# Conditioning matmuls of a decoder block in whole visits from a ring of their own

## The chip, the cores and the metric

One core of a Trainium2 chip runs the whole kernel. The metric is the device time of one execution in microseconds (us); lower is better. The times before are 1353.8, 1354.12 and 1354.7 us, with a median of 1354.12. All views below are of one other execution, taken by the hardware profiler: it took 1353.11 us, of which 1351.3 us lie between its first and its last instruction (the span).

## The reference, cut to what matters

One layer of a decoder trunk runs on 288 token columns: 256 of a prompt, and 32 of eight samples with four tokens each. All numbers are 32-bit floats.

```
mod = silu(c) @ w_ada + b_ada            # 9 conditions; 6 parts of 2048 columns: sh1 sc1 g1 sh2 sc2 g2
h   = rmsnorm(x)*(1+sc1) + sh1
proj = h @ w_in                          # pooling input u, gate z, xbc (conv + state-space mixer), dt
mix = concat(pool(u), ssd(z, xbc, dt)) @ w_out
x   = x + g1*mix
h2  = rmsnorm(x)*(1+sc2) + sh2
x   = x + g2*((silu(conv(h2 @ w_gate)) * (h2 @ w_val)) @ w_down)
y   = rmsnorm(x)
```

The change is about the first line, the conditioning. It multiplies nine condition vectors by a 2048 x 12288 matrix, 100 MB to be read. Parts 0 and 1 (sh1, sc1) are needed first. Parts 2, 3 and 4 (g1, sh2, sc2) are needed at the output projection and behind it. Part 5 (g2) comes still later.

## The kernel before, in words

Every weight comes from HBM by a DMA that SyncE (SP) issues, mostly 512 KB at a time, into a buffer named `raw` (`load`, L267). A large weight is then split for accuracy into a high part `whi` (ScalarE, ACT) and a rest `wlo` (VectorE, DVE) by `split` (L293). TensorE (PE) runs three matmuls for each 128 x 128 block of it on all 288 columns (`mm3`, L301).

**The rings.** A ring is a fixed number of buffers that loads take in turn; a load waits until the last reader of its buffer is done. Class `_W` (L457) keeps one ring of `raw`, one of `whi` and one of `wlo`, and gives them buffers as memory comes free. Pool `w1` (L485) gives 8 `raw` and 2 of each split buffer for the whole run. Pool `w0` (L502) gives 8 and 1 until the last block of the input projection. Pool `w2` (L1156) gives 1 and 2 from step m == 5 of the output stage on. Conditioning loads and weight loads share the `raw` ring.

**The stages.** Blocks 0 to 5 of the input projection run first, with parts 0 and 1 of the conditioning between them (`ada_group_units`, L352). The last block (bi = 6, 28 steps m) makes the rest of `xbc`. The uz stage (L1038) then makes the remaining z and u in eight steps of eight units. Beside it runs the state-space mixer of four head groups (`back`), whose many small matmuls take turns with the large ones on PE. The output stage (L1087 and L1151) has sixteen steps of 48 large matmuls. The MLP follows.

**The conditioning matmuls.** `ada_part_units` (L405) makes one part. For each of 16 slices k of the contraction it loads two chunks of 512 KB and runs four matmuls with 32 columns of weights and 512 columns of data (`ada_mm`, L329). Each of the four has a quarter of the PE array, so that four run side by side. The data is plain fp32 here, not split. A matmul in the program is two matmul records in the profile. With AY = 2 the generator hands back control after every second k, so a part is eight visits of 8 matmuls (16 records). Behind the last, ACT copies the sums out (`ada_sb`, L335), PE transposes them (`ada_tr`, L340), and four DVE instructions add the bias (L420).

**What sets the order.** The program is one list of instructions, and generators place the conditioning between other work: `pull` (L987) counts up a fraction at each step and asks for the next piece when it reaches one. The last block pulls 0.25 a step (L1033), uz 0.2 a unit (L1043); two visits are pulled behind uz (L1051). The output stage pulls 0.5 and later 1 a step (L1167), and what is left is drained at m == 13 (L1169). At build time the framework's scheduler then orders each engine's queue: by program order, but an instruction whose inputs it takes to be late may be overtaken by one that it takes to be ready. `tc.high_priority()` lets an instruction go ahead of others, and `tc.keep_in_program_order` sets it behind the instruction before it on its engine. Parts 0 and 1 use both (L377 to L382), parts 2 to 5 neither. On the chip each engine runs its queue strictly in the order that was fixed.

Of the kernel before, what the change touches and what calls it, by code (L numbers as in the profile page):

```python
# [39 lines left out]
RAW0, RAW1, RAW2 = 8, 8, 1  # L40
# [11 lines left out]
AY = 2  # L52

RA1, RA2, RB1, RB2, RB3 = 0.5, 0.4, 1.0, 1.0, 1.0
TA, ADA_OUT = 4, 4
# [109 lines left out]
def kernel(ctx: ExitStack, tc, ins, outs):  # L165
# [101 lines left out]
    def load(key):  # L267
        off, cols = S.items[key]
        t = wp[0].tile([P, RAWC], F32, tag="raw", name="raw_" + "_".join(map(str, key)))
        nc.sync.dma_start(t[:, :cols], wflat[off:off + P * cols].rearrange("(p n) -> p n", p=P))  # L270
        return t
# [5 lines left out]
    def top_up():  # L277

        while queue and nloads[0] - min((n for n, _ in ahead.values()), default=nloads[0]) < RAW0 + RAW1:
            key = queue.popleft()  # L280
            ahead[key] = (nloads[0], load(key))
            nloads[0] += 1
# [121 lines left out]

    def ada_part_units(part, ay=1):  # L405
        ps = pa.tile([P, 512], F32, tag="ada", name=f"adap{part}")
        for k in range(KT):
            raws = [load(("adap", part, k, h)) for h in range(2)]
            for h in range(2):
                ada_mm(ps, raws[h], k, 0, 512, range(2 * h, 2 * h + 2))  # L410
            if k % ay == ay - 1:
                yield
        asb = ada_sb(ps, 512, f"p{part}")
        yield
        pt = ada_tr(asb, 512, f"p{part}")
        for i in range(4):
            o = ada[:, part].rearrange("p (j i) c -> p j i c", j=4)[:, :, i, :]
            b = bada[:, part].rearrange("p (j i) -> p j i", j=4)[:, :, i]
            src = pt[:, i * P:(i + 1) * P].rearrange("p (j c) -> p j c", j=4)[:, :, 0:NC9]
            nc.vector.tensor_tensor(o, src, b.unsqueeze(2).to_broadcast([P, 4, NC9]), ALU.add)  # L420
        if part == 4:
            ada_scale(1, 4, vec[:, V_N2:V_N2 + KT], 0, KT)
        yield
# [33 lines left out]
    class _W:  # L457


        def __init__(self):  # L460
            self.slots = {"raw": [], "whi": [], "wlo": []}
            self.i = {"raw": 0, "whi": 0, "wlo": 0}

        def add(self, pool, nraw, nsp):
            for tag, n in (("raw", nraw), ("whi", nsp), ("wlo", nsp)):
                m = len(self.slots[tag])
                if m:
                    r = self.i[tag] % m
                    self.slots[tag] = self.slots[tag][r:] + self.slots[tag][:r]
                    self.i[tag] = 0  # L470
                self.slots[tag] += [(pool, n)] * n

        def drop(self, pool):
            for tag, sl in self.slots.items():
                r = self.i[tag] % len(sl)
                self.slots[tag] = [x for x in sl[r:] + sl[:r] if x[0] is not pool]
                self.i[tag] = 0

        def tile(self, shape, dt, tag, name):
            pool, n = self.slots[tag][self.i[tag] % len(self.slots[tag])]  # L480
            self.i[tag] += 1
            return pool.tile(shape, dt, tag=tag, name=name, bufs=n)

    wp[0] = _W()
    wp[0].add(ctx.enter_context(tc.tile_pool(name="w1", bufs=1, side="right")), RAW1, SPLIT1)  # L485
# [16 lines left out]
    wp[0].add(w0, RAW0, SPLIT0)  # L502
# [405 lines left out]
    adas = chain(*(ada_part_units(p, AY) for p in (2, 3, 4)))  # L908
# [86 lines left out]
    for bi in range(len(BLOCKS)):  # L995
        last = bi + 1 == len(BLOCKS)
        top_up()
        if last:

            wp[0].drop(w0)  # L1000
            w0_ctx.close()
            sx[0] = mx_ctx.enter_context(tc.tile_pool(name="sx", bufs=1, reuse_waits="tile"))
            raw = load(("dt",))[:, :KT * NH].rearrange("p (k h) -> p k h", h=NH)
# [11 lines left out]
            late_states()  # L1015
            dt_stage(ps)
# [4 lines left out]
        for i, m in enumerate(xbc_units(bi)):  # L1021
            if not last:
                top_up()
                if bi == 0 and i in (3, 7, 13):
                    ci = {3: 2, 7: 3, 13: 4}[i]
                    ready["xbc", 0, ci] = split(fetch(("xbc", 0, ci)), 0, len(_xbc_chunks(0)[ci][1]) * P,
                                                f"xbc0_{ci}", pin=True)
                if i in VIS[bi]:
                    next(nxt)
                    top_up()  # L1030
            else:
                pull(back, 0.5 if m < 20 else RB1) if m >= 9 else None
                pull(adas, RA1 / AY)  # L1033
# [4 lines left out]
    for m in list(range(4 + 3 * ZEARLY, 16)) + ULATE:  # L1038
        for _ in uz_units(m):
# [3 lines left out]
            pull(adas, RA2 / AY)  # L1043
# [7 lines left out]
    pull(adas, TA / AY)  # L1051
# [36 lines left out]
    for i in range(KT // YK):  # L1088
# [6 lines left out]
        if i == 3:  # L1095
            psq = aux("ysum")
            col_sums(psq, ssq, ones[:, 0:1], True, True)
            _, rstdy = rstd_of(psq, NH * 64, "rstdy")
    mx_ctx.close()
# [51 lines left out]
    for m in range(16):  # L1151
# [15 lines left out]
        pull(adas, (1 + (m >= 14 - ADA_OUT)) / AY)  # L1167
# [3 lines left out]

    adag2 = ada_part_units(5)
# [285 lines left out]
```

## Time and profile before

| what | value |
|---|---|
| median of three runs | 1354.12 us (1353.8 to 1354.7) |
| the profiled execution | 1353.11 us |
| its span | 1351.3 us |
| last block of the input projection | from about 189 to 257 us |
| uz stage with the mixer | about 257 to 373 us |
| output stage | about 373 to 495 us |
| DMA reads from HBM | 309.78 MB |

PE rows are matmuls, PEld rows are weight loads into the array, which overlap them; SPq rows are DMA issues. A row of the timeline gives the start, the time until the end of its last matmul, engine, line, operation, output <- inputs, shapes and the count of like instructions in a row. Matmuls are pipelined, so rows overlap a little, and the distance from start to start is the true step. In a wait table the waiter stands left of the arrow. Rows of "windows" give the busy time of each engine in a stretch, with the count of instructions.

### The profile page before, as it was taken

How to read it: one execution, taken by the hardware profiler on the slowest of the kernel's cores; microseconds unless marked ns; L12 is line 12 of the kernel's file. 1: busy time of each engine (PE TensorE's matmuls, PEld its weight loads, DVE VectorE, ACT ScalarE, POOL GpSimd, SP SyncE). 2: the span in 40 equal slices, each digit the busy share in tenths (PEclk: the TensorE clock that was granted, in tenths of full speed). 3: DMA queues.
4: the chain of work that ended last, by engine and by line, in shares of the span. 5: the costliest groups of instructions: out<-in, count | busy, mean ns of one | idle time of the engine just before them, and what ended most of it. 6: DMA issues, size and time to landing. Idle time of an engine off the chain costs nothing.

```text
span 1351.3 us, 26246 instructions
## 1 busy us (share of the span) xinstructions
PE 1337.3 (99%) x10517; PEld 1247.5 (92%) x10517; DVE 820.0 (61%) x1394; ACT 579.4 (43%) x911; POOL 227.5 (17%) x449
## 2 busy tenths in 40 slices
PE   9999999999999999999999999999999999999997
PEld 8889997776789889999999999999999999999997
DVE  5776568778665568645665445656655556566543
ACT  5343244587733335434443333434433343444442
POOL 0000012122122223111211001321120011132221
PEclk9999999999999999999999999999999999999999
DMA  9999768978888877787555555655555565566531
GB/s 373 405 408 368 252 242 324 340 257 295 324 332 323 320 253 257 249 280 265 181 187 182 162 178 183 204 183 196 181 180 164 184 191 184 187 207 194 179 119 70
DMA packets 97482, 323.19 MB, mean 239 GB/s; under 512 B 10768, under 2 KB 19920, under 8 KB 97360
## 3 DMA queue, kind: packets, MB, share of 16 engines
q1 hardware_dynamic: 93600, 310.79, 66.3%
q0 software_dynamic: 3184, 9.69, 2.0%
q8 instruction: 82, 1.34, 0.4%
q10 hardware_dynamic: 576, 1.03, 0.2%
q14 instruction: 40, 0.33, 0.1%
HBM read 309.78 MB, written 10.39 MB: 237 GB/s over the span
## 4 chain that ended last, share of the span: by engine, by line
PE 74%; DVE 1%; issue 0%; ACT 0%; DVEq 0%
PE mm_down L304 7%; PE mm_down L303 7%; PE mm_down L305 7%; PE mm_gate L303 6%; PE mm_val L304 6%; PE mm_gate L304 6%; PE mm_val L305 6%; PE mm_gate L305 6%; PE mm_val L303 6%; PE adap L332 3%; PE mm_out L303 2%; PE mm_out L304 2%; PE mm_out L305 2%; PE mm_up L303 1%; PE mm_up L304 1%; PE mm_up L305 1%
## 5 line engine op out<-in xcount | busy, mean ns | idle before, releaser
L304 PE MATMUL mm_down<-al,whi_down 128*128 128x288 f32 x688 | 202.5, 294 | 0.0
L303 PE MATMUL mm_down<-ah,whi_down 128*128 128x288 f32 x688 | 202.4, 294 | 0.0
L305 PE MATMUL mm_down<-ah,wlo_down 128*128 128x288 f32 x688 | 202.0, 294 | 0.0
L304 PE MATMUL mm_val<-h2l,whi_val 128*128 128x288 f32 x640 | 189.1, 296 | 0.0
L304 PE MATMUL mm_gate<-h2l,whi_gate 128*128 128x288 f32 x640 | 189.1, 295 | 0.0
L303 PE MATMUL mm_gate<-h2h,whi_gate 128*128 128x288 f32 x640 | 188.8, 295 | 0.0
L305 PE MATMUL mm_val<-h2h,wlo_val 128*128 128x288 f32 x640 | 188.4, 294 | 0.0
L305 PE MATMUL mm_gate<-h2h,wlo_gate 128*128 128x288 f32 x640 | 188.4, 294 | 0.0
L303 PE MATMUL mm_val<-h2h,whi_val 128*128 128x288 f32 x640 | 187.9, 294 | 0.0
L291 DVE TENSOR_TENSOR wlo_gate<-raw_gate,whi_gate 128x1024 fp32r<-128x1024 f32 x80 | 98.4, 1230 | 136.4 <-ACT whi_gate L289 136.3
L291 DVE TENSOR_TENSOR wlo_down<-raw_down,whi_down 128x1024 fp32r<-128x1024 f32 x96 | 107.5, 1120 | 116.9 <-ACT whi_down L289 114.4
L289 ACT CAST whi_down<-raw_down 128x1024 fp32r<-128x1024 f32 x96 | 92.3, 961 | 167.0 <-PE mm_down L304 118.0
L289 ACT CAST whi_gate<-raw_gate 128x1024 fp32r<-128x1024 f32 x80 | 83.8, 1049 | 160.0 <-PE mm_gate L304 64.9
L289 ACT CAST whi_val<-raw_val 128x1024 fp32r<-128x1024 f32 x80 | 84.1, 1051 | 119.5 <-issue 101.9
L303 PE MATMUL xbc<-h1h,whi_xbc 128*128 128x288 f32 x448 | 133.5, 301 | 0.8 <-ACT h1h L453 0.7
L304 PE MATMUL xbc<-h1l,whi_xbc 128*128 128x288 f32 x448 | 132.0, 296 | 0.0
L305 PE MATMUL xbc<-h1h,wlo_xbc 128*128 128x288 f32 x448 | 130.0, 295 | 0.0
L303 PEld LDWEIGHTS mm_down<-ah,whi_down 128*128 128x128 f32 x688 | 129.2, 188 | 0.0
L304 PEld LDWEIGHTS mm_down<-al,whi_down 128*128 128x128 f32 x688 | 129.1, 188 | 0.0
L305 PEld LDWEIGHTS mm_down<-ah,wlo_down 128*128 128x128 f32 x688 | 129.0, 187 | 0.0
L303 PEld LDWEIGHTS mm_gate<-h2h,whi_gate 128*128 128x128 f32 x640 | 120.3, 188 | 5.0 <-ACT ah L1221 3.4
L305 PEld LDWEIGHTS mm_gate<-h2h,wlo_gate 128*128 128x128 f32 x640 | 120.5, 188 | 0.0
(331 smaller groups left out, 2994.8 us busy)
## 6 DMA issues: line engine op xcount, KB each, us to landing
raw_adap<-wflat SPq DMA_DIRECT2D x128, 512.0 KB, 5.6
raw_gate<-wflat SPq DMA_DIRECT2D x80, 512.0 KB, 3.6
raw_val<-wflat SPq DMA_DIRECT2D x80, 512.0 KB, 3.9
raw_ada<-wflat SPq DMA_DIRECT2D x64, 512.0 KB, 9.6
raw_xbc<-wflat SPq DMA_DIRECT2D x50, 512.0 KB, 9.5
raw_down<-wflat SPq DMA_DIRECT2D x48, 512.0 KB, 3.6
raw_out<-wflat SPq DMA_DIRECT2D x32, 512.0 KB, 7.6
raw_down<-wflat SPq DMA_DIRECT2D x32, 384.0 KB, 3.1
```

Of the source, the lines that this page charges most:

```text
L289: yield nc.scalar.copy(hi[:, :n], raw[:, a:a + n])
L291: yield hi, lo, nc.vector.tensor_tensor(lo[:, :n], raw[:, a:a + n], hi[:, :n].bitcast(F32), ALU.subtract)
L303: nc.tensor.matmul(ps, whi[:, w], bh, start=first, stop=False)
L304: nc.tensor.matmul(ps, whi[:, w], bl, start=False, stop=False)
L305: nc.tensor.matmul(ps, wlo[:, w], bh, start=False, stop=last)
L332: nc.tensor.matmul(ps[32 * j:32 * j + 32, :nb], sc_c[:, k, :], raw[:, c:c + nb], start=(k == 0), stop=(k == KT - 1), tile_position=(0, 32 ...
```

## The change

Parts 2, 3 and 4 get a new generator, `ada_visits`. It loads all chunks of a visit, hands back control, and then puts all matmuls of the visit in one piece: the first waits for the chunk that was loaded last, the others have high priority, and all are kept in program order. A visit of parts 2 and 3 holds two slices k (AK = 2: 4 chunks, 8 matmuls, as before). A visit of part 4 holds four (AK2 = 4: 8 chunks, 16 matmuls), so part 4 has four visits in place of eight.

The chunks of these parts get a ring of their own, `rawa`. In the first blocks its four buffers of `w1` still count to the common ring (4 + 4 + 8 buffers, as before). From the last block on they are `rawa`, and weights have four of `w1` and one in pool `sx`, five, in place of eight shared. In the output stage `rawa` has eight buffers, and weights four, in place of nine shared; the additional split buffers come at m == 0 in place of m == 5. For the MLP all twelve are one ring, in place of nine.

Parts 2 and 3 are pulled at 4 x 5.01/28 a step in the last block and 4 x 11.01/62 a unit in uz, with four pulls to a visit: 5 visits and 11. Part 4 runs at the ends of steps 3, 6, 9 and 12 of the output stage; its chunks are asked for one by one in the two steps before each. Nothing is pulled behind uz as a block of its own. The four bias additions of a part become one DVE instruction at high priority, for part 5 too.

```diff
-RAW0, RAW1, RAW2 = 8, 8, 1
+RAW0, RAW1, RAWA, RAW2 = 8, 4, 4, 4
-AY = 2
-RA1, RA2, RB1, RB2, RB3 = 0.5, 0.4, 1.0, 1.0, 1.0
-TA, ADA_OUT = 4, 4
+VA = (5.01 / 28, 11.01 / 62)
+AK, AK2, AOUT = 2, 4, (3, 6, 9, 12)
+RB1, RB2, RB3 = 1.0, 1.0, 1.0
...
+    def ada_visits(parts, step, spread=False):
+        plan = [(part, k0) for part in parts for k0 in range(0, KT, step)]
+        ahead, end = [], None
+        def chunks(v):
+            part, k0 = plan[v]
+            for k in range(k0, k0 + step):
+                for h in range(2):
+                    ahead.append((k, h, load(("adap", part, k, h), "rawa")))
+                    if spread:
+                        yield
+            if not spread:
+                yield
+                yield
+        yield from chunks(0)
+        for v, (part, k0) in enumerate(plan):
+            if end:
+                ada_end(*end)
+                end = None
+            if k0 == 0:
+                ps = pa.tile([P, 512], F32, tag="ada", name=f"adap{part}")
+            n = 0
+            for k, h, raw in ahead[::-1]:
+                for j in (2 * h, 2 * h + 1):
+                    with tc.high_priority() if n else nullcontext():
+                        i = nc.tensor.matmul(ps[32 * j:32 * j + 32, :], sc_c[:, k, :],
+                                             raw[:, 512 * (j % 2):512 * (j % 2) + 512], start=k == step - 1,
+                                             stop=k == KT - step, tile_position=(0, 32 * j))
+                    tc.keep_in_program_order(i)
+                    n += 1
+            ahead.clear()
+            if k0 + step == KT:
+                end = part, ada_sb(ps, 512, f"p{part}")
+            yield
+            if not spread:
+                yield
+            if v + 1 < len(plan):
+                yield from chunks(v + 1)
+        ada_end(*end)
+        yield
...
+    def ada_end(part, asb):
         pt = ada_tr(asb, 512, f"p{part}")
-        for i in range(4):
-            o = ada[:, part].rearrange("p (j i) c -> p j i c", j=4)[:, :, i, :]
-            b = bada[:, part].rearrange("p (j i) -> p j i", j=4)[:, :, i]
-            src = pt[:, i * P:(i + 1) * P].rearrange("p (j c) -> p j c", j=4)[:, :, 0:NC9]
-            nc.vector.tensor_tensor(o, src, b.unsqueeze(2).to_broadcast([P, 4, NC9]), ALU.add)
+        with tc.high_priority():
+            nc.vector.tensor_tensor(ada[:, part].rearrange("p (j i) c -> p i j c", j=4),
+                                    pt.rearrange("p (i j c) -> p i j c", i=4, j=4)[:, :, :, 0:NC9],
+                                    bada[:, part].rearrange("p (j i) -> p i j", j=4).unsqueeze(3)
+                                    .to_broadcast([P, 4, 4, NC9]), ALU.add)
...
-    adas = chain(*(ada_part_units(p, AY) for p in (2, 3, 4)))
+    adas = ada_visits((2, 3), AK)
...
             wp[0].drop(w0)
+            wp[0].move("rawa", "raw", "rawa")
...
+            wp[0].add(sx[0], "raw", "raw", 1)
...
             late_states()
+            next(adas)
             dt_stage(ps)
...
-                pull(adas, RA1 / AY)
+                pull(adas, 4 * VA[0])
...
-            pull(adas, RA2 / AY)
+            pull(adas, 4 * VA[1])
...
-    pull(adas, TA / AY)
+    drain(adas)
...
+    wp[0].drop(sx[0])
     mx_ctx.close()
...
-        if m == 5:
-            wp[0].add(w2, RAW2, SPLIT2)
+        if m == 0:
+            for tag, n in (("rawa", RAW2), ("whi", SPLIT2), ("wlo", SPLIT2)):
+                wp[0].add(w2, tag, tag, n)
+            adas = ada_visits((4,), AK2, True)
...
+                if i % 2 and m < AOUT[-1] and m % 3:
+                    next(adas)
...
-        pull(adas, (1 + (m >= 14 - ADA_OUT)) / AY)
+        if m in AOUT:
+            next(adas)
         if m == 13:
             drain(adas)
+    wp[0].move("rawa", "rawa", "raw")
```

The rest of the diff lets `load` name its ring and rewrites class `_W` so that a buffer can be moved from one ring to another.

More of the change, by code (lines that the diff above doesn't have):

```diff
@@ L277, in top_up @@
     def top_up():
-        while queue and nloads[0] - min((n for n, _ in ahead.values()), default=nloads[0]) < RAW0 + RAW1:
+        while queue and nloads[0] - min((n for n, _ in ahead.values()), default=nloads[0]) < RAW0 + RAW1 + RAWA:
             key = queue.popleft()
@@ L460, in __init__, with turn, add, move @@
         def __init__(self):
[L461 to L471, printed above, removed]
+            self.slots = {"raw": [], "rawa": [], "whi": [], "wlo": []}
+            self.i = dict.fromkeys(self.slots, 0)
+        def turn(self, ring):
+            sl = self.slots[ring]
+            r = self.i[ring] % len(sl) if sl else 0
+            self.slots[ring], self.i[ring] = sl[r:] + sl[:r], 0
+        def add(self, pool, ring, tag, n):
+            self.turn(ring)
+            self.slots[ring] += [(pool, tag, n)] * n
+        def move(self, tag, a, b):
+            self.turn(a)
+            self.turn(b)
+            self.slots[b] += [x for x in self.slots[a] if x[1] == tag]
+            self.slots[a] = [x for x in self.slots[a] if x[1] != tag]
         def drop(self, pool):
[L474 to L477, printed above, removed]
+            for ring in self.slots:
+                self.turn(ring)
+                self.slots[ring] = [x for x in self.slots[ring] if x[0] is not pool]
         def tile(self, shape, dt, tag, name):
-            pool, n = self.slots[tag][self.i[tag] % len(self.slots[tag])]
-            self.i[tag] += 1
+            pool, tag, n = self.slots[tag][self.ix(tag)]
             return pool.tile(shape, dt, tag=tag, name=name, bufs=n)
+        def ix(self, ring):
+            self.i[ring] += 1
+            return (self.i[ring] - 1) % len(self.slots[ring])
     wp[0] = _W()
-    wp[0].add(ctx.enter_context(tc.tile_pool(name="w1", bufs=1, side="right")), RAW1, SPLIT1)
+    w1 = ctx.enter_context(tc.tile_pool(name="w1", bufs=1, side="right"))
+    for ring, tag, n in (("raw", "raw", RAW1), ("raw", "rawa", RAWA), ("whi", "whi", SPLIT1), ("wlo", "wlo", SPLIT1)):
+        wp[0].add(w1, ring, tag, n)
     mx_ctx = ExitStack()
@@ L501 @@
     shift(w0, 32)
-    wp[0].add(w0, RAW0, SPLIT0)
+    for tag, n in (("raw", RAW0), ("whi", SPLIT0), ("wlo", SPLIT0)):
+        wp[0].add(w0, tag, tag, n)
     sx = [None]
```

7 lines of the change are left out of this document (4 added, 3 removed).

## The prediction

> **What bounds the kernel now.** I read the page first, then the waits of PE between 196 and 501 us, where parts 2 to 4 of the conditioning run.
>
> ```profile
> PE 1337.3 (99%) x10517; PEld 1247.5 (92%) x10517; DVE 820.0 (61%) x1394; ACT 579.4 (43%) x911; POOL 227.5 (17%) x449
> ...
> PE 74%; DVE 1%; issue 0%; ACT 0%; DVEq 0%
> ```
> ```profile
> PE cse L801 <- DVE ada L420: 1.0, 1, 1.0
> PE pool L888 <- DVE pout L883: 0.8, 1, 0.8
> PE dttr L582 <- DVE dtt L570: 0.6, 1, 0.6
> PE cb L751 <- DVE xde L740: 0.3, 1, 0.3
> ```
>
> PE is busy for 99% of the span and names the chain that ended last. In these 305 us it waits 2.7 us in four places, and never for a DMA. So no stall of size is to be had. Time can only come from PE work that takes longer than it must: matmuls that don't fill the array, and changes between kinds of matmul. The question is how much of that the conditioning contains, and whether the new rings turn a wait for a DMA into PE time. First a visit that is in one piece, in the output stage:
>
> ```profile
> 397.60 0.29 PE L305 MATMUL mm_outp<-mixh,wlo_out 128*128 128x288 f32 x1
> 397.82 1.92 PE L332 MATMUL adap<-raw_adap,sc_c 128*32 128x512 f32 x16
> 399.68 0.40 PE L303 MATMUL mm_out<-mixh,whi_out 128*128 128x288 f32 x1
> 399.92 0.30 PE L304 MATMUL mm_out<-mixl,whi_out 128*128 128x288 f32 x1
> ```
>
> The visit takes 1.86 us from start to start. From 397.60 to 399.92 are 2.32 us, where two steps of large matmuls would be 0.26 (they follow each other by 0.13). A visit thus costs 2.06 us, of which 0.20 are entry and exit. Now one in uz that the build order has cut in two, and the first piece of another that is cut in three:
>
> ```profile
> 324.92 1.04 PE L332 MATMUL adap<-raw_adap,sc_c 128*32 128x512 f32 x2
> ...
> 332.85 1.92 PE L332 MATMUL adap<-raw_adap,sc_c 128*32 128x512 f32 x14
> ```
> ```profile
> 213.97 1.05 PE L332 MATMUL adap<-raw_adap,sc_c 128*32 128x512 f32 x2
> ```
>
> This is the main reading. Two records alone take 1.04 us, and the fourteen left take 1.92, as long as sixteen. Four matmuls side by side take as long as one, so a piece that isn't a multiple of eight records pays for a whole round of the array, about 0.9 us. From this first one on seven visits are cut, one in three and six in two: eight pieces too many. The last of them is quoted further down, with the joint behind uz.
>
> **The change part by part.** *Tying.* The busy time of these matmuls by stretch:
>
> ```profile
> 196.00:373.00 177.00, 38.44 (x268) 7.72 (x272) 1.18 (x2) 1.00 0.83 305
> 373.00:501.00 128.00, 20.95 (x160) 4.27 (x152) 0.58 (x1) 1.00 0.83 310
> ```
> ```profile
> 496.40 1.04 PE L332 MATMUL adap<-raw_adap,sc_c 128*32 128x512 f32 x2
> ...
> 498.17 2.77 PE L332 MATMUL adap<-raw_adap,sc_c 128*32 128x512 f32 x22
> ```
>
> Together 59.39 us. The first part of part 5 is in it and stays (1.92 + 1.04 + 2.77 = 5.73). The 24 visits of parts 2 to 4, whole, would be 24 x 1.92 = 46.08. The excess is 7.58; the eight pieces overlap what follows by some 0.07 each, which leaves **-7.0**. Each piece also has an entry and exit, 0.2 beside large matmuls and nothing beside other small ones; I take 0.1: **-0.8** (0 to -1.6). That the tie holds is read from the stage before, where parts 0 and 1 have it:
>
> ```profile
> 48.14 1.93 PE L378 MATMUL adag<-raw_ada,sc_c 128*32 128x256 f32 x32
> ```
>
> It is the first of twelve such visits up to the dt stage; each is one row of 32 in the timeline.
>
> *Four long visits.* The row of 22 records is three rounds, so a round is 2.77 - 1.92 = 0.85 us. Four rounds take 3.62, or 3.75 with the overlap taken off and the entry added. Eight visits of 2.05 (16.4) become four of 3.75 (15.0): **-1.4**.
>
> *One addition in place of four.* PE's 1.0 us wait above is for the last of them:
>
> ```profile
> 285.87 0.39 DVE L420 TENSOR_TENSOR ada<-adat_p,early 128x36 f32<-128x36 f32 x3
> ```
>
> The last three of the four stand behind others on DVE, and the PSUM bank that they read is held until the fourth is through. A single one at the head of the queue frees it sooner by at most the wait, 1.0; I take **-0.7** (0 to -1.0), nearer to the whole since nothing is left behind the first. DVE is 61% busy, so the twelve instructions less (0.13 each by this row, part 5 included) give nothing else.
>
> *What goes from the joint behind uz.* Two visits now stand between uz and the output stage, as rows of PE and one of DVE show:
>
> ```profile
> 371.11 0.29 PE L305 MATMUL mm_uz<-h1h,wlo_uz 128*128 128x288 f32 x1
> 371.25 0.60 PE L343 MATMUL adat_p<-early,asb_p 128*128 128x128 f32 x4
> 371.77 1.93 PE L332 MATMUL adap<-raw_adap,sc_c 128*32 128x512 f32 x16
> ```
> ```profile
> 378.59 1.04 PE L332 MATMUL adap<-raw_adap,sc_c 128*32 128x512 f32 x2
> 379.57 0.75 PE L888 MATMUL pool<-pout,poolw 128*128 128x288 f32 x2
> 380.15 0.72 PE L241 MATMUL ysum<-ones,ssq 128*128 128x1 f32 x6
> 380.81 1.92 PE L332 MATMUL adap<-raw_adap,sc_c 128*32 128x512 f32 x14
> ```
> ```profile
> 378.53 0.17 DVE L883 TENSOR_TENSOR pout<-pout,upp 128x16 f32<-128x16 f32 x1
> ```
>
> The last uz matmul is at 371.1; the pooling that hangs on it leaves DVE at 378.7. Between lie 36 large matmuls, and three pieces of conditioning, 4.7 us from start to start, that cover the rest. Without them the large ones end near 376.5, and PE has 2.2 us until the pooling can go on, unless weights of the next step are split by then (their buffers come free after 24 of the 36). I take **+2.0**; the bounds are 0 and the whole cover, 4.7.
>
> *A ring of one visit.* `rawa` holds four chunks, which is just one visit: a load waits on SP until the visit before has read its buffer. What is queued behind it on SP are loads of weights; what is queued behind a visit on PE is everything. How long does a batch take to come? Twice from SP's timeline, each with the landing of its last load from the DMA view of that instant:
>
> ```profile
> 398.92 1.75 SPq L270 DMA_DIRECT2D raw_adap<-wflat  x4
> ```
> ```profile
> raw_adap<-wflat SPq DMA_DIRECT2D x1, 512.0 KB, 6.0
> ```
> ```profile
> 226.86 0.80 SPq L270 DMA_DIRECT2D raw_adap<-wflat  x2
> 227.77 0.84 SPq L270 DMA_DIRECT2D raw_xbc<-wflat  x2
> 228.67 7.39 SPq L270 DMA_DIRECT2D raw_adap<-wflat  x4
> ```
> ```profile
> raw_adap<-wflat SPq DMA_DIRECT2D x1, 512.0 KB, 9.1
> ```
>
> The visit at 397.82 frees its buffers, four loads follow, the last is issued at 400.3 and lands 6.0 later: 8.5 us from visit to full ring. With two weight loads between (the visit at 225.77, fourth load at 229.2, landing 9.1 later) it is 12.5. The visits' distance comes from the stage rows:
>
> ```profile
> 189.00:257.00 68.00, 67.40 (x510) 53.66 (x512) 58.61 (x138) 31.56 (x45) 15.65 (x31) 1.00 0.83 307
> 257.00:373.00 116.00, 113.89 (x916) 83.28 (x912) 82.98 (x161) 88.50 (x199) 24.57 (x35) 1.00 0.82 297
> ```
>
> The last block loses two of its seven visits and a cut: near 63 us, 28 steps, a visit every 5.6: 12.5 us. uz has eleven, near 112 us for 64 units, a visit every 5.6: 9.9 us. So the last block has room, and uz lies between the two reload times. The build order lets other matmuls go first where it sees the batch late; PE stops only by what the chip is later than it. I take **+1.0**, with 0 below; the other end is a rival. The weights' smaller rings I price at nothing: uz uses one 512 KB load in 7 us and has five buffers, the output stage one in 3.2 us with four, 12.7 us of cover, and four split buffers behind. A load there takes 7.6 (median):
>
> ```profile
> raw_out<-wflat SPq DMA_DIRECT2D x32, 512.0 KB, 7.6
> ```
>
> If that cover goes, each late load stops PE for what it is late. Part 4's eight chunks have three steps of 6.3 us and a visit, 22.8 us. Two loads more made 4.0 us of the two reload times, so eight take at most 8.5 + 4 x 2.0 = 16.5 by themselves.
>
> *Sum.* -7.0 - 0.8 - 1.4 - 0.7 + 2.0 + 1.0 = **-6.9 us**. The profiled execution took 1353.1 and would take 1346.2. It lies 1.0 below the median of 1354.1, so I forecast **1347.2**.
>
> **The rivals.** *1. The ring that is reloaded too late (slower).* In uz each visit stands at the head of PE's queue before its last chunk has landed. At 12.5 us of reload against 9.9 of distance, eleven visits wait up to 2.6 each: 28 us. At half of that 14 us, and 1361. It eats the gain from 0.7 us of wait per uz visit on ((6.9 + 1.0) / 11). For it: 297 GB/s already move in that stage, and one batch has no second buffer. Against it: PE waited for no DMA before, and a visit may be moved back. The Trainium skill, Trainium Kernel Development and Optimization, section Best Practices, says: "Double-buffer for performance: Overlap DMA with compute". By that rule a ring of exactly one visit is the wrong size, and this rival would be the likeliest; no row here shows such a ring yet.
>
> *2. The gain is given back at the joint.* The full 4.7 us of cover are missed, and the other terms hold: -4.2, 1349.9. For it: the pooling chain of 7.3 us behind uz (371.4 to 378.7) is DVE's, and nothing in the change shortens it. Against it: weights of step 1 may be ready.
>
> *3. It doesn't do what it says.* New pins move the cuts elsewhere, into the mixer's small matmuls, and pieces stay. Then only the long visits and the joint count, about 0: 1354. Against it is the row of 32.
>
> *4. More than counted.* The joint costs nothing, no batch is late, every entry counts: -7.0 - 1.6 - 1.4 - 1.0 = -11.0, 1343.1.
>
> **How the numbers follow.** Forecast 0.60, its own range 1344 to 1351; rival 1 0.16; rival 2 0.12; rival 3 0.07; rival 4 0.05. The range of 1343 to 1356 leaves out half of rival 4 and most of rival 1. A measurement of this kernel tells about 0.2% from no change, 2.7 us, so faster means below 1351.4 and slower above 1356.8. Faster: the forecast nearly whole, rival 4, half of rival 2: 0.71. Same: the rest of rival 2, most of 3, the mild part of 1: 0.14. Slower: 0.15.
>
> **What would show it.** Right: visits as single rows of 16 (1.9 us) and four rows of 32 (3.6) after each third output step; busy time of these matmuls near 51 us between 196 and 501; no wait of DVE's addition; a gap of up to 2 us before the pooling behind uz. Wrong: waits of PE for a chunk, or of the `whi` casts for weights that then reach PE; rows of 2 or 6 records; visits that slip behind uz.

## The result, and the profile after

The changed kernel takes 1357.69 us (median of 16 runs, 1355.96 to 1359.64), the kernel before beside it 1353.70 us (16 runs, 1352.58 to 1354.70). The ratio is 1.003, with a 95% interval of 1.0023 to 1.0038. The change makes the kernel slower by about 4 us, where 1347.2 had been forecast. The profiled execution took 1357.75 us, of which 1355.9 are the span.

First come the two lines of the page after that answer to those of before: busy time, and the chain that ended last.

```profile
PE 1332.5 (98%) x10517; PEld 1247.9 (92%) x10517; DVE 823.0 (61%) x1382; ACT 577.8 (43%) x909; POOL 222.0 (16%) x449
...
PE 90%; DMA 5%; DVE 2%; ACT 1%; SPq 1%; issue 1%; POOL 0%; DVEq 0%; ACTq 0%; POOLq 0%
```

PE is busy for 4.8 us *less* in a span that is 4.6 us longer. So matmul time has gone, and more than that has come as waiting. DMA, which the chain of before did not name, has 5% of the chain. The wait table of PE between 180 and 520 us says where:

```profile
PE mm_out L303 <- ACT whi_out L289: 4.2, 2, 2.2
PE mm_out L305 <- DVE wlo_out L291: 3.3, 4, 1.5
PE adap L432 <- DMA raw_adap<-wflat: 1.2, 2, 1.0
PE pool L946 <- DVE pout L941: 1.1, 2, 0.7
PE cb L809 <- DVE xde L798: 0.8, 2, 0.6
PE cse L859 <- DVE yo L845: 0.4, 1, 0.4
```

The first two rows did not exist before: large matmuls of the output stage wait 7.5 us for the casts that split a weight. The wait of `cse` for the bias addition (`ada`, 1.0) is gone.

What the change did to the visits stands in PE's timeline (start, us, count at the end of the row):

```profile
357.70 1.92 PE L432 MATMUL adap<-raw_adap,sc_c 128*32 128x512 f32 x16
367.45 1.92 PE L432 MATMUL adap<-raw_adap,sc_c 128*32 128x512 f32 x16
...
401.12 3.64 PE L432 MATMUL adap<-raw_adap,sc_c 128*32 128x512 f32 x32
404.69 0.40 PE L303 MATMUL mm_out<-mixh,whi_out 128*128 128x288 f32 x1
```

Every visit of parts 2 and 3 is one row of 16, from 194.75 to 367.45 us, and part 4 is four rows of 32 that take 3.57 us from start to start. Their busy time, in two stretches that meet between two visits (the first number behind the comma is PE's; 1.00 and 0.99 are the mean granted TensorE clock, as a share of the full one):

```profile
194.00:365.00 171.00, 28.86 (x240) 6.26 (x240) 0.59 (x1) 1.00 0.82 301
365.00:505.00 140.00, 22.34 (x184) 5.28 (x184) 1.18 (x2) 0.99 0.86 311
```

That is 51.2 us against 59.39 before. The same from start to start, without the overlaps, gives an account of all that lies between the first matmul of the dt projection and the first of the MLP (`mm_up`). A large matmul follows another by 0.1321 us where nothing is late; what a stretch of them takes beyond that is its loss.

| us | before | after | difference |
|---|---|---|---|
| whole stretch | 315.51 | 319.81 | +4.30 |
| conditioning matmuls, part 5's first pieces among them | 56.93 | 50.04 | -6.9 |
| losses of large matmuls ahead of the output stage | 11.09 | 11.04 | 0.0 |
| losses of large matmuls in the output stage | 1.87 | 12.10 | **+10.2** |
| all other matmuls | 44.77 | 45.80 | +1.0 |

The losses stand in two places: 6.3 us at 385 to 395 us (steps 2 and 3 of the stage), and 4.3 us at 421 and at 441 to 445. (Elsewhere the stage loses a little less than before, since it has fewer visits.) Follow three of the waits back. PE's timeline (in brackets the idle time before a row and what ended it):

```profile
387.44 0.40 PE L303 MATMUL mm_out<-mixh,whi_out 128*128 128x288 f32 x1 [2.05 <-ACT whi_out L289]
...
389.34 0.44 PE L304 MATMUL mm_out<-mixl,whi_out 128*128 128x288 f32 x1
389.58 0.44 PE L305 MATMUL mm_out<-mixh,wlo_out 128*128 128x288 f32 x1
...
394.83 0.40 PE L305 MATMUL mm_out<-mixh,wlo_out 128*128 128x288 f32 x1 [1.54 <-DVE wlo_out L291]
...
443.45 0.40 PE L303 MATMUL mm_out<-mixh,whi_out 128*128 128x288 f32 x1 [2.20 <-ACT whi_out L289]
```

The two rows in the middle wait for nothing, yet follow each other by 0.24 us in place of 0.13. The window of PE there shows why: the granted clock is half.

```profile
388.50:391.70 3.20, 3.00 (x12) 0.50 1.03 401
```

For 3.4 us, from 388.4 on, thirteen large matmuls run at half clock, which costs 1.5 us. So the loss of 12.1 us in the output stage is 7.5 us of waits, 1.5 us of half clock, and 3.1 us in small pieces at waits and visits, where the kernel before has 1.9 in all. The waits came first, and without the stretch at half clock this execution would still have taken about 1356 us. The sixteen executions differ in their mean clock: the six at 0.996, the profiled one among them, took 1355.96 to 1357.75 us, the eight at 0.994 took 1357.68 to 1359.64, and those of the kernel before that ran beside the experiments stand at 0.997 or 0.998. That the slower ones had a further such stretch is not shown, as only one execution was profiled.

ACT's timeline shows that the casts had no choice either; they waited for the load:

```profile
386.34 1.04 ACT L289 CAST whi_out<-raw_out 128x1024 fp32r<-128x1024 f32 x1 [0.37 <-DMA raw_out<-wflat]
...
419.25 1.05 ACT L289 CAST whi_out<-raw_out 128x1024 fp32r<-128x1024 f32 x1 [6.40 <-DMA raw_out<-wflat]
...
442.36 1.04 ACT L289 CAST whi_out<-raw_out 128x1024 fp32r<-128x1024 f32 x1 [5.95 <-DMA raw_out<-wflat]
```

And SP's timeline shows what those loads stood behind, at the start of the stage and after the first long visit:

```profile
368.55 3.10 SPq L270 DMA_DIRECT2D raw_adap<-wflat  x5
371.70 0.95 SPq L1216 DMA_DIRECT2D x<-x  x2
...
373.28 0.40 SPq L270 DMA_DIRECT2D raw_out<-wflat  x1
...
402.21 6.60 SPq L270 DMA_DIRECT2D raw_adap<-wflat  x8
408.91 13.00 SPq L270 DMA_DIRECT2D raw_out<-wflat  x5
```

The code asks for the eight chunks of a visit one by one over two steps. But behind the long visit they stand in SP's queue as one row of eight, ahead of the weights, and go out from 402.21 to 408.16, as the visit at 401.12 frees the buffers. (At the start of the stage it is six chunks and two loads of `x` ahead of the weight at 373.28.) The landing times of the trace: the chunk issued last, at 408.16, lands at 417.87, and the weight issued at 408.91 lands at 419.15. The next three weights land at 420.43, 421.69 and 422.95, one in every 1.27 us. The DMA view of the five weights:

```profile
raw_out<-wflat SPq DMA_DIRECT2D x5, 512.0 KB, 10.1
```

Their median is 10.1 us from issue to landing, where the stage before the change had a median of 7.6. Between 403.64 and 419.15 us no weight lands at all; 15.5 us are nearly five weights' worth of matmuls (one in 3.2 us). Ahead of the two larger groups of waits the gaps are longer: 18.4 us (367.96 to 386.32) and 17.2 us (425.03 to 442.26). Behind the visit at 450.99 the gap is 12.4 us (454.93 to 467.33), less than four weights' worth, and no large matmul waits.

### The profile page after: what moved, and what is told of

Same layout as the page of the kernel before. It is cut to its first block, busy times and chain, and to the rows that moved or that the text cites. A ratio compares the mean times of both kernels' runs of the same rounds, so it can differ in the third digit from the quotient of the medians.

```text
span 1355.9 us, 26197 instructions
## 1 busy us (share of the span) xinstructions
PE 1332.5 (98%) x10517; PEld 1247.9 (92%) x10517; DVE 823.0 (61%) x1382; ACT 577.8 (43%) x909; POOL 222.0 (16%) x449
## 3 DMA queue, kind: packets, MB, share of 16 engines
HBM read 309.78 MB, written 10.39 MB: 236 GB/s over the span
## 4 chain that ended last, share of the span: by engine, by line
PE 90%; DMA 5%; DVE 2%; ACT 1%; SPq 1%; issue 1%; POOL 0%; DVEq 0%; ACTq 0%; POOLq 0%
PE mm_down L304 7%; PE mm_down L303 7%; PE mm_down L305 7%; PE mm_gate L303 6%; PE mm_val L304 6%; PE mm_gate L304 6%; PE mm_gate L305 6%; PE mm_val L305 6%; PE mm_val L303 6%; PE xbc L303 5%; PE xbc L304 4%; PE xbc L305 4%; PE adap L432 3%; DMA raw_out<-wflat 2%; PE adag L378 2%; DMA raw_adap<-wflat 1%
```

## The experiments

The theory: the large matmuls lose time because eight chunk loads go out in one burst ahead of a weight on the one queue, and the rest of the change gives what was forecast. The rivals were that the new ring or the new distances cost something by themselves, that the weights have too few buffers, that SP's standing in the queue (not the bytes) delays the weights, and that visits of eight chunks cost something whatever the order. All ratios are against the kernel before, run beside each.

**part4_as_before.** Part 4 goes back to short visits of four chunks at the old pace, from one common ring, with the additional split buffers at m == 5; parts 2 and 3 stay as changed.

```diff
-            adas = ada_visits((4,), AK2, True)
+            adas = ada_part_units(4, 2)
...
-        if m in AOUT:
-            next(adas)
+        pull(adas, (1 + (m >= 10)) / 2)
...
+    wp[0].move("rawa", "rawa", "raw")
```

> Parts 2 and 3 as in the changed kernel; part 4 as in the kernel before: visits of two slices, four chunks each, from a ring that they share with the weights (8 buffers, 9 from step 5 on, with the additional split buffers from step 5). Theory (the burst of eight chunks after each long visit stands ahead of the weights in the DMA queue, and a ring of four for the weights can't cover it): no wait of PE for a weight cast in the output stage, and what the tied visits won up to the end of uz is left, 4 to 5 us: about 1349. Rival (what uz wins is only work that was moved behind it): 1353 to 1354.

1347.59 us, ratio 0.9955 (0.9941 to 0.9969): 5.9 us below the kernel before, and the fastest of all kernels here. The two largest waits of PE from 180 to 520 us:

```profile
PE pool L946 <- DVE pout L941: 1.1, 2, 0.7
PE adap L432 <- DMA raw_adap<-wflat: 1.0, 1, 1.0
```

No large matmul waits for a cast. Their loss in the output stage is 2.33 us, and the conditioning takes 49.99. SP issues four chunks and then four weights:

```profile
395.70 3.19 SPq L270 DMA_DIRECT2D raw_adap<-wflat  x4
398.98 5.46 SPq L270 DMA_DIRECT2D raw_out<-wflat  x4
```

So the loss came with the long visits, and not from the ring or the distances of parts 2 and 3. Which property of the long visits it is, this run alone does not say: it changes their length, their ring and their place.

**short_visits.** The generator, the ring of eight and the split buffers of the change stay; a visit of part 4 holds two slices in place of four, pulled evenly.

```diff
-AK, AK2, AOUT = 2, 4, (3, 6, 9, 12)
+AK, AK2 = 2, 2
...
-                if i % 2 and m < AOUT[-1] and m % 3:
-                    next(adas)
+                pull(adas, 0.39)
...
-        if m in AOUT:
-            next(adas)
```

> The changed kernel with part 4 in eight visits of two slices, evenly over steps 1 to 13; rings as in the changed kernel (eight buffers for chunks, four for weights). A visit frees four buffers, so bursts are half as long, 5 us, but as many bytes are moved. Theory (length of the burst): most waits go, 1347 to 1350, with 1.4 us more for the four additional visits. Rival (ring of four, or total load on the DMA): 1355 or more.

1348.85 us, ratio 0.9964 (0.9951 to 0.9978). The waits for casts are gone, the loss in the output stage is 2.33 us. Ring and split buffers are thus cleared; what is left is the batch of eight, or its place, which changes with it.

**no_reload.** The first visit of part 4 loads its eight chunks, the other three use them again.

```diff
-                    ahead.append((k, h, load(("adap", part, k, h), "rawa")))
+                    ahead.append((k, h, load(("adap", part, k, h), "rawa") if not spread or v == 0
+                                  else kept[len(ahead)][2]))
...
+            kept[:] = ahead
```

> The changed kernel, but visits 2 to 4 of part 4 read the first batch's buffers again: 24 of part 4's 32 chunks aren't loaded (part 4 comes out as another number). Theory of the burst: the waits in the output stage from step 4 on go (0.8 and 3.5 us in the trace), those of the first steps (6.3 us) stay, since the first batch is loaded as before: 1353 to 1354. Rival (four buffers are too few for the weights whatever else is loaded): all waits stay, 1357.

1353.55 us, ratio 0.9997 (0.9988 to 1.0007). From 400 us on no large matmul waits for a cast; what stays is the group at 385 to 393:

```profile
PE mm_out L305 <- DVE wlo_out L291: 2.0, 2, 1.5
PE mm_out L303 <- ACT whi_out L289: 1.8, 1, 1.8
```

The loss falls from 12.10 to 6.17 us (the profiled execution has no stretch at half clock, which is 1.5 us of the difference). The two groups are thus separate: the later one belongs to the three reloads, the early one to the first batch, which this kernel still loads.

**tiny_reload.** The reloads stay in the queue in their places and with their waits, but move only 16 columns of each chunk (8 KB in place of 512; the visits use the first visit's data).

```diff
+                    if spread and v:
+                        raw = kept[len(ahead)][2]
+                        nc.sync.dma_start(raw[:, :16], wflat[S.items["adap", part, k, h][0]:][:P * 16]
+                                          .rearrange("(p n) -> p n", p=P))
+                    else:
+                        raw = load(("adap", part, k, h), "rawa")
```

> The changed kernel, but the chunk loads of visits 2 to 4 of part 4 move 16 columns in place of 1024 into the same buffers (the rest stays from the first batch; part 4 comes out as another number). SP still waits for the visit before each of them, with the weights queued behind. If the transfer time of the burst delays the weights: as without the reload, 1353 to 1354. If SP's standing wait does: the waits from step 4 on stay, 1356 to 1358.

1352.57 us, ratio 0.9992 (0.9983 to 1.0001), as fast as without the reloads. SP's timeline after the first long visit:

```profile
401.67 3.66 SPq L416 DMA_DIRECT2D raw_adap<-wflat  x8
405.43 3.94 SPq L270 DMA_DIRECT2D raw_out<-wflat  x4
```

Eight issues still stand ahead of the weights, and after 400 us no large matmul waits for a cast. So it is the time that the bytes of the eight take on the queue, not the issuing.

**first_batch_later.** The long visits come after steps 4, 7, 10 and 13, and the first eight chunks are asked for in steps 2 and 3, pinned to their places in the queue.

```diff
-AK, AK2, AOUT = 2, 4, (3, 6, 9, 12)
+AK, AK2, AOUT = 2, 4, (4, 7, 10, 13)
...
+        if pin:
+            tc.keep_in_program_order(i)
...
-                    ahead.append((k, h, load(("adap", part, k, h), "rawa")))
+                    ahead.append((k, h, load(("adap", part, k, h), "rawa", spread and v == 0)))
...
-                if i % 2 and m < AOUT[-1] and m % 3:
+                if i % 2 and 1 < m < AOUT[-1] and m % 3 != 1:
```

> The changed kernel with part 4 one step later throughout (visits behind steps 4, 7, 10 and 13), and the first batch's loads held on SP behind the weights of the steps before. Theory: the 6 us of waits in steps 2 to 4 come from the first batch and the x loads being ahead of the weights of step 2; they go, and the later ones (4 us) stay or move: 1352 to 1354. Rival (the start suffers from the split buffers or from the memory that becomes free late): they stay, 1357.

1352.85 us, ratio 0.9997 (0.9988 to 1.0006). Of the early group 1.6 us are left (at 378 to 380), the later one has 4.2 (442 to 448, of which 1.5 at half clock). It is the counterpart of no_reload: most of each half can be taken away alone.

**weights_ring8.** Four more weight buffers in the output stage, in the memory of the two additional split buffers.

```diff
-            for tag, n in (("rawa", RAW2), ("whi", SPLIT2), ("wlo", SPLIT2)):
+            for tag, n in (("rawa", RAW2), ("raw", 4)):
```

> The changed kernel with eight buffers for the weights in the output stage in place of four, paid with the two additional split buffers of each kind (memory holds no more): the bursts stay as they are. Theory (burst and small ring together): eight halves are 25 us of matmuls, more than the 10 us that a burst takes, so nearly all waits go: 1347 to 1350. Rival (the loss hangs on the split buffers or on the order of the first steps): waits stay or grow, 1356 or more.

1361.56 us, ratio 1.0061 (1.0047 to 1.0075). This missed. The waits stand in nearly the same places, 0.5 to 1.6 us at a time, and the loss in the output stage is 11.15 us in place of 12.10; 4.4 us of it lie at 439 to 446, of which 1.5 at half clock. SP's timeline says why buffers do no good:

```profile
401.23 6.21 SPq L270 DMA_DIRECT2D raw_adap<-wflat  x8
407.54 5.35 SPq L270 DMA_DIRECT2D raw_out<-wflat  x5
413.79 0.33 SPq L1216 DMA_DIRECT2D x<-x  x1
424.26 6.36 SPq L270 DMA_DIRECT2D raw_adap<-wflat  x8
430.72 8.52 SPq L270 DMA_DIRECT2D raw_out<-wflat  x8
```

Weights now go out early, by 412.9 us. But the next in the queue are the eight chunks of the next visit, which wait for the visit at 424: SP stands still for 10 us with weight buffers free, and the weights behind go out at 430.72 and land from 440.12. Deeper buffers can't help a load that stands behind a waiting one in a queue. That it is even 4 us slower than the changed kernel does not come from here: from dt to the MLP it takes 319.13 us, 0.7 less. Behind the MLP's start it takes 7.1 us more (its profiled execution, at 1364.21 us, is the slowest of its four), and PE waits there for casts in places where the changed kernel waits for none:

```profile
PE mm_val L305 <- DVE wlo_val L291: 1.8, 2, 0.9
PE mm_val L303 <- ACT whi_val L289: 1.0, 1, 1.0
```

The two split buffers of each kind that this kernel gives up are missing in the MLP too, which would explain it; that wasn't tried apart.

**interleaved.** The chunk loads and the weights of the output stage are pinned in the order in which the code asks for them, weights two steps ahead.

```diff
+    def preload(m, h):
+        if m < KT:
+            pre[m, h] = load(("out", m, h), pin=True)
...
+            for mh in ((1, 0), (1, 1), (2, 0), (2, 1)):
+                preload(*mh)
...
+            preload(m + 2, 0)
             for i, (pz, pp) in enumerate(out_units(m)):
+                if i == 3:
+                    preload(m + 2, 1)
```

> The changed kernel, rings and visits as they are, but on SP the output stage's loads stand in a written order: weights two steps ahead of their use, and one or two chunks of part 4 between each two of them, so that no eight chunks go ahead of a weight. Theory (order of the burst against the weights): the 10 us of waits of the large matmuls in the output stage go, and with the long visits it stands a little below part_4_as_before: 1346 to 1348. Rival (a ring of four for the weights is too small under this load, in whatever order): over 1353.

1354.10 us, ratio 1.0006 (0.9997 to 1.0015). Half a hit: behind 390 us no large matmul waits, though all eight chunks of each visit are loaded. But a new wait has come at the start of the stage:

```profile
PE mm_out L305 <- ACT whi_out L291: 2.5, 1, 2.5
```
```profile
364.00 16.57 SPq L270 DMA_DIRECT2D raw_out<-wflat  x3
380.67 0.37 SPq L270 DMA_DIRECT2D raw_adap<-wflat  x1
```

The first row is of the wait table, the others of SP's timeline. The pinned weights of later steps wait for buffers, and SP issues nothing from 368.0 until 380.2; large matmuls lose 5.3 us at 375 to 386, 1.5 of them at half clock.

**order_and_late.** Both cures together: the late visits of first_batch_later, and the order of interleaved from step 4 on.

```diff
-            for mh in ((1, 0), (1, 1), (2, 0), (2, 1)):
-                preload(*mh)
...
-            preload(m + 2, 0)
+            if m > 1:
+                preload(m + 2, 0)
...
-                if i == 3:
+                if i == 3 and m > 1:
                     preload(m + 2, 1)
```

> Both halves of the cure in one kernel: the four long visits come one step later (after steps 4, 7, 10 and 13, their first eight chunks spread over steps 2 and 3), and from step 4 on the queue order of chunk loads and weights is the written one, the weights of a step asked for two steps ahead; steps 1 to 3 load their weights as in the changed kernel. If a late weight, and nothing else, is what the changed kernel loses, then both groups of waits go and the time is the changed kernel's less their 10.2 us, 1346 to 1348.5 us (ratio 0.9945 to 0.996), with no wait of a large matmul for a cast over 1 us in the output stage. If visits of eight chunks cost something by themselves (the bytes of eight chunks have to pass in three steps, whatever their order), waits move to another step and the time stays at 1351 or more.

1357.16 us, ratio 1.0026 (1.0017 to 1.0035): a miss. Again no large matmul waits behind 404 us, and 9.6 us are lost at 380 to 404: 5.7 in waits, 3.1 in two stretches at half clock. SP's timeline there:

```profile
378.43 0.86 SPq L270 DMA_DIRECT2D raw_adap<-wflat  x2
385.39 1.46 SPq L270 DMA_DIRECT2D raw_out<-wflat  x2
```

The weights of step 4 were asked for ahead of those of step 3 and took their buffers; SP issued nothing from 379.3 to 385.4 us. The one execution of eleven at the mean clock of the kernel before, 0.998, took 1354.49 us; the others, at 0.994 to 0.996, took 1355.2 to 1358.75.

**order_after_start.** As order_and_late, but step 2 asks for the weights of steps 3 and 4 in their own order, and the order of two steps ahead begins at step 3.

```diff
-            if m > 1:
+            if m > 2:
                 preload(m + 2, 0)
...
-                if i == 3 and m > 1:
+                if i == 3 and m > 2:
                     preload(m + 2, 1)
+                if i == 5 and m == 2:
+                    for mh in ((3, 0), (3, 1), (4, 0), (4, 1)):
+                        preload(*mh)
```

> order_and_late kept the waits of 380 to 400 us because the weights of step 4 were asked for ahead of those of step 3 and held their buffers, so that SP stood from 379.4 to 385.4 us. Here step 2 asks for the weights of steps 3 and 4 in their own order, and the written order of two steps ahead begins at step 3; the visits stay after steps 4, 7, 10 and 13. If a late weight is all that the changed kernel loses, both groups of waits are gone now: 1346 to 1348.5 us (ratio 0.9945 to 0.996). If eight chunks at a time cost something by themselves, some of the waits come back at another step, and the time is 1351 or more.

1349.48 us, ratio 0.9972 (0.9961 to 0.9982). Of the waits of PE from 180 to 520 us, the largest and the only one of the output stage's large matmuls:

```profile
PE adap L434 <- DMA raw_adap<-wflat: 1.4, 2, 1.0
...
PE mm_out L307 <- DVE wlo_out L293: 1.0, 1, 1.0
```

Four visits of eight chunks, as in the changed kernel, and a loss in the output stage of 3.05 us in place of 12.10, half of it around one wait at 380. No stretch of the stage is at half clock. SP's timeline behind the first long visit shows the difference to the changed kernel:

```profile
405.47 0.33 SPq L270 DMA_DIRECT2D raw_adap<-wflat  x1
405.89 0.38 SPq L270 DMA_DIRECT2D raw_out<-wflat  x1
406.36 1.35 SPq L270 DMA_DIRECT2D raw_adap<-wflat  x3
407.80 0.42 SPq L270 DMA_DIRECT2D raw_out<-wflat  x1
```

So visits of eight chunks need not make a weight late: the rival that they cost something whatever the order falls, and the order of the queue decides. The time is 1 us above the expected range. From dt to the MLP this kernel takes as long as part4_as_before (309.77 and 309.78 us); the 2 us between their spans lie outside, 0.5 ahead of dt and 1.5 behind the MLP's start. Of the 1.5 us, 1.3 are one wait of `mm_up` at 501.96 for ACT's `h2h`; why that comes later stays open, as do the 0.5. The intervals of the two ratios overlap.

**ties_only.** The kernel before, with loads of a visit first and its matmuls tied as in the change; no ring, no distances, no long visits, four additions.

```diff
+            for q, h, raw in raws[::-1] if ay > 1 else raws:
+                for j in (2 * h, 2 * h + 1):
+                    with tc.high_priority() if n and ay > 1 else nullcontext():
+                        i = nc.tensor.matmul(ps[32 * j:32 * j + 32, :], sc_c[:, q, :],
+                                             raw[:, 512 * (j % 2):512 * (j % 2) + 512], start=q == ay - 1,
+                                             stop=q == KT - ay, tile_position=(0, 32 * j))
+                    if ay > 1:
+                        tc.keep_in_program_order(i)
```

> The kernel before with nothing but the ties: a visit of parts 2 to 4 keeps its two slices, its shared ring and its place, but its matmuls stand in one piece (last chunk first, high priority, program order). The prediction's first term says -7.0 and -0.8 us: about 1346. If the even distances and the ring of their own are what brings the win up to uz's end, it is less than half of that: 1351 or more.

1350.96 us, ratio 0.9981 (0.9972 to 0.999). Six of the seven cut visits are whole, and the conditioning takes 52.06 us, 4.9 less than before. One visit stays in pieces, in PE's timeline among the dt transposes:

```profile
213.59 1.05 PE L413 MATMUL adap<-raw_adap,sc_c 128*32 128x512 f32 x4
214.57 0.24 PE L589 MATMUL dttr<-early,dtt 24*128 24x24 f32 x1
214.74 1.04 PE L413 MATMUL adap<-raw_adap,sc_c 128*32 128x512 f32 x2
...
215.88 1.05 PE L413 MATMUL adap<-raw_adap,sc_c 128*32 128x512 f32 x2
...
217.02 1.06 PE L413 MATMUL adap<-raw_adap,sc_c 128*32 128x512 f32 x8
```

Pieces of 2, 4 and 8 records last the same, 1.04 to 1.06 us. The four take 3.94 us from start to start where a whole visit takes 1.85. In the changed kernel the visits stand at 206.32 and 219.16, on both sides of the transposes. So of the 7.0 us of cuts the tie alone wins 4.9, and 2.1 need the new places. But the kernel is only 2.5 us faster, where the prediction's first terms would give 1346: this was a miss. From dt to the MLP it takes 3.0 us less, as the matmuls that are neither large nor conditioning take 1.5 us more and the large ones lose 0.4 more.

## Why the prediction was wrong, point by point

The direction was wrong, and one term of the sum did it.

- **The step that failed**: "The weights' smaller rings I price at nothing". The runs put +10.2 us in its place. The working behind it compared a load's 7.6 us with a cover of 12.7, and the cover was counted rightly. But 7.6 was measured where chunks go out four at a time. The prediction itself worked out a line later that eight chunks take up to 16.5 us, and held this against the 22.8 us that the *chunks* have, never against the 12.7 that the *weights behind them* have. The 16.5 was right (the trace has 16.8, from the visit at 401.12 to the last landing at 417.87). It is more than 12.7, and there was the loss. A weight that is issued right behind the eight takes 10.2 us (and the one at 373.28, with two loads of `x` ahead as well, 13.0), to which the time that it stood unissued is to be added. The prediction did name waits for the `whi` casts among the signs of being wrong, but gave them no price.
- **What no term held**: 1.5 us of the 10.2 are half clock. In these twelve traces, leaving out the first and the last 10 us, such stretches of 3.4 us stand only in kernels whose large matmuls wait for late weights. Each begins at most 1.1 us behind the end of a wait, and the waits just ahead of it come to 1.9 to 3.2 us. The kernels in which no large matmul waits over 1.0 us for a weight have none. Not every wait is followed by one: none comes in no_reload, and none behind the wait of 2.2 us at 443 in the changed kernel. That the waits bring them on is thus likely, but not shown.
- **What was read from the code and not from the queue**: that the chunks are "asked for one by one in the two steps before". Behind the long visits they go out eight in a row, since the build order moved them together and one visit frees all their buffers. interleaved and order_after_start keep them apart, and behind the first long visit no large matmul waits.
- *Tying*, -7.0: right in size. The excess over whole visits was 7.0 before (56.93 less 24 x 1.85 and 5.54 of part 5) and is 0 after. But ties_only shows that only 4.9 of it is the tie, the rest is where the visits stand, and that 1.9 of the 4.9 came back in other matmuls.
- *Entries and exits*, -0.8: not to be seen; losses of large matmuls ahead of the output stage are 11.09 and 11.04.
- *Four long visits*, -1.4: right by its parts, not seen in the time. In order_after_start against part4_as_before, 4 x 3.57 against 8 x 1.85 is -0.5, and four entries of 0.2 fewer would be -0.8. The two kernels take equally long there, as the one late weight left costs about as much.
- *One addition*, -0.7: the wait of 1.0 is gone, but other small waits grew (`cb` 0.3 to 0.8, `pool` 0.8 to 1.1, `cse` for `yo` 0.4), and all other matmuls take 1.0 us longer. It need not be the addition or the rings: ties_only, which has neither, shows 1.5 us of the kind. Part 5's first pieces became four in place of three, +0.6.
- *The joint behind uz*, +2.0: nothing. The last visit of part 3 slipped to 367.45, into the first output step, and the pooling behind uz, now at 371.17, waits for nothing; the longest wait of `pool` is 0.7 at 334 us (0.8 before).
- *The ring of one visit*, +1.0: right, 1.2 us in two waits for `raw_adap`.
- **The rivals.** The first had the sign and the kind of cause, a load that comes too late, and the wrong ring: the chunks in uz, where 1.2 us was all. By the rule that it named (the Trainium skill, Trainium Kernel Development and Optimization, section Best Practices, on double-buffering) the chunk ring of one visit was the fault, and these traces disagree: that ring costs 1.2 us, and the rule says nothing of a second ring on the same queue. Nearer to the cause is the Trainium skill, DMA: Bandwidth & Descriptors, section Queues, rings and completion order: on each DMA engine descriptors are consumed in ring order, though completion in the order of issue is not promised. The trace agrees with the first: the 512 KB loads of SP's queue land in the order of their issue, 1.27 us apart behind the visit at 401.12.
- With the late weights taken away, the sum comes out near: part4_as_before, all of the change but the long visits, is at 1347.59 us, where the forecast without its -1.4 for the long visits is 1348.6. That agreement is partly luck, since +2.0 and -0.8 that didn't come and +1.6 that did weigh each other up.

## What to carry to other kernels

A cover counted in buffers (so many loads times the time of one's use) holds only for a load that goes out when its buffer is free; ask what stands ahead of it in its queue, and add the bytes of the largest batch there to its landing time. When a change makes batches larger, hold the time of a batch against the cover of *every* ring that shares the queue. And where loads are meant to be spread, look at the order of the issuing engine's queue, not at the loop that asks for them; if it matters, pin it, for all the loads that share the buffers, from a point at which the buffers are really free.

## What the runs showed of the hardware that was not expected

- Loads of 512 KB that stand in a row on SP's queue land at a steady distance, chunks and weights alike: 1.27 us each, about 410 GB/s. A load right behind eight others takes 10.2 us; the median with batches of four was 7.6 in the kernel before and 7.1 in part4_as_before.
- Eight loads of 16 columns in the same places delay nothing that PE feels (tiny_reload), though their issues take 3.66 us of SP's time.
- Four more weight buffers took only 1 us off the loss in the output stage (weights_ring8), as the loads that could fill them stood behind loads that could not go out.
- A late weight can cost more than its wait. The granted clock fell to 0.50 for 3.4 us behind some groups of waits of 1.9 us or more, and large matmuls then followed each other by 0.24 us in place of 0.13, 1.5 us a time. In order_and_late two such stretches make 3.1 of 9.6 us.
